# A decoder layer on one NeuronCore: reversed queries with bias tiles read from the head's own row, two accumulating transfers tied to a later split, and a sum of squares on another engine

## The chip, the cores and the metric

The kernel runs on one core of a Trainium2 chip. The metric is the device time of one execution in microseconds, the median of several runs. The core has five engines that run their own instruction streams: TensorE (PE, matmuls; PEld is its weight load), VectorE (DVE), ScalarE (ACT), GpSimd (POOL) and SyncE (SP), which only issues transfers. Transfers run on 16 DMA engines that serve several queues: q0 is fed by POOL, q1 by SP, q10 by ACT. Engines wait for each other through semaphores. On each engine the instructions are carried out in the order in which they stand.

## The reference, cut to what matters

One layer: a SwiGLU feed-forward block with a factor 0.5, a mixer (a Mamba-2 group beside differential attention with a relative position bias), cross-attention into a memory of 256 tokens, a second feed-forward block, and norms between. 512 tokens, width 1024, 8 attention heads with two queries and keys of 64 each.

```python
qb = jnp.moveaxis(q.reshape(bsz, nb, Q_BLOCK, nh, 2, dh), 1, 0)      # Q_BLOCK = 128
...
    rel = k_pos[None, :] - q_pos[:, None]
    bias = jnp.transpose(rel_bias[rel_bucket(rel)], (2, 0, 1)).astype(jnp.float32)
    logits = jnp.einsum('bqhcd,bkhcd->bhcqk', q_blk, k) * scale
    logits = jnp.where(rel[None, None, None] <= 0, logits + bias[None, :, None], -jnp.inf)
    p = jax.nn.softmax(logits, axis=-1)
    w = p[:, :, 0] - lam * p[:, :, 1]
    return jnp.einsum('bhqk,bkhe->bqhe', w.astype(v.dtype), v)
...
y = y + d_skip[:, None] * xh                                         # Mamba-2 group
y = y.reshape(bsz, seqlen, SSD_WIDTH) * jax.nn.silu(z)
yg = y.reshape(bsz, seqlen, SSD_GROUPS, SSD_WIDTH // SSD_GROUPS)
yg = yg * lax.rsqrt(jnp.mean(yg * yg, axis=-1, keepdims=True) + EPS)
...
x = x + 0.5 * swiglu(rms_norm(x, norm_ffn1_w[l]), ffn1_w_in[l], ffn1_w_out[l])
```

The bias depends on the distance between query and key alone, so a head's bias is one row of 512 values by distance.

## The kernel before

Every dense product runs as three matmuls on operands split into a high and a low part: ACT writes the high part (`wh`, L155), DVE subtracts it and writes the low part (`wl`, L156), and PE multiplies high x high, high x low and low x high. Weights come from DRAM through SP into one of six buffers `wr` (512 KB each), are split into one of three `wh` and three `wl` buffers, and are used by PE. The feed-forward products use Strassen's scheme in Winograd's form on blocks of weights (B11, B12, B21, B22) and of activations.

PE, DVE and ACT are ordered by a scheduler when the program is built; SP and POOL carry out their instructions in the order in which the program writes them down. The work is written as generators that an `Order` object advances: dense products in sequence, and chains of small steps between them. `behind(list)` makes an instruction wait for the ones in the list.

**`out_blocks`** is the second matrix of a feed-forward block, for a third of its rows. It runs seven block products: `a` with B11, `e` with the first weight sum, `b` with the second weight sum (activations S2), `a` again with B21, `b` with `sums[1]` and the activations S3, `e` with B22 and S4, and `b` with the fourth weight sum and the blocks called "22". Each has two parts (`parts`), each part one weight tile and four steps of six matmuls in all two accumulators. In the first feed-forward block the weight sums are formed on the fly. The first three share one buffer per part, `t_raw[part]`: B12 + B11 by an accumulating transfer that POOL issues (L1320), then + B22 by DVE (L1330), then + B21. In the last third (`by_dma`) that last addition is an accumulating transfer too, `t4` (L1341), issued by POOL for both parts after the S3 product has been written down. `sums[1]`, B12 + B22, is an accumulating transfer of its own per part (L1320), into a `wr` buffer for the first part and into the tile `gate` for the second. Right behind `t4` on POOL's queue stands a small power (`ncol`, L363) for the memory's norm. Meanwhile SP fetches the weights of the memory's keys (`in_wck`).

**The bias.** `prepare` forms a table `rel_d` in DRAM, 8 rows of 640 values, one row for each head: 512 by falling distance and 128 of a large constant for masked keys. A row's window that starts at 127 - p is what query p of a block of 128 needs. `expand_bias` writes a head's row 128 times into `rel_z`, in rows of 641; `ask_bias` reads it back with a step of 640, so that partition p gets the window at 127 - p. The first two heads' expansions are issued by ACT in `prepare`, behind recent splits (L640 at 323.6 and 332.6 us), the other six by SP in `queries_keys` (L640 from 348.8 to 537.6 us). The bias tile is added to the scores on DVE (L776).

**Queries and head outputs.** `queries_keys` projects a head's query, splits it from PSUM with the factor -1 (`q`, L159 on ACT and L160 on DVE), then projects and splits the key, and spawns `head`, where the queries are the stationary operand of the scores. At its end the head's output is transposed back to channels x tokens in PSUM (`pot`) and split into `ya`, which `out_attn` multiplies.

**`group`** is one of four groups of the Mamba-2 part. Its two gated tiles are squared on ACT (`ysq`, L1003), POOL adds the two squares (L1005), PE sums over channels (`pn`), and DVE and POOL form the norm's row. POOL also issues the accumulating transfers that form the second feed-forward block's weight sums in DRAM (`isum`, `wsum`, L1266); some stand behind the add on its queue.

Of the kernel before, what the change touches and what calls it, by code (L numbers as in the profile page):

```python
# [11 lines left out]
F32 = mybir.dt.float32  # L12
R32 = mybir.dt.float32r
AF = mybir.ActivationFunctionType
ALU = mybir.AluOpType
AX = mybir.AxisListType

P = 128
T = 512
# [12 lines left out]
RW = 640  # L32
# [68 lines left out]
def body(tc, a, dbg=None):  # L101
    nc = tc.nc
# [8 lines left out]
    dram = ctx.enter_context(tc.tile_pool(name="dram", bufs=1, space=bass.MemoryType.DRAM))  # L111
# [7 lines left out]
    def s2(s, dt=F32, shape=(P, T)):  # L119
        if math.prod(shape[1:]) <= T // 2:  # L120
            return sp.tile(list(shape), dt, tag="s1", name=nm(s), bufs=NHALF)
        return sp.tile(list(shape), dt, tag="s2", name=nm(s))
# [4 lines left out]
    def small(s, n, bufs=None):  # L127
        return tiny.tile([P, n], F32, tag=s, name=nm(s), bufs=bufs)

    def acc(s, shape=(P, T)):  # L130
        return acc_p.tile(list(shape), F32, tag="acc", name=nm(s))

    def aux(s, shape=(P, T)):
        return aux_p.tile(list(shape), F32, tag="aux", name=nm(s))
# [5 lines left out]
    last, start, last_sum, recent, newest, newest_mm = [], [], [], [], [], []  # L140
    V, S, G = nc.vector, nc.scalar, nc.gpsimd
    od = Order()

    def mm(out, w, x, start, stop):
        od.t += (1 if w.dtype == R32 else 4) * (x.free_size() + 8) / 2400
        newest_mm[:] = [nc.tensor.matmul(out, w, x, start=start, stop=stop).ins]  # L146
# [5 lines left out]
    def split_into(hi, lo, src, scale=None):  # L152
        if scale is None:
            return (
                S.activation(hi, src, AF.Copy),  # L155
                V.tensor_tensor(lo, src, hi.bitcast(F32), ALU.subtract),  # L156
            )
        return (
            S.activation(hi, src, AF.Copy, scale=scale),  # L159
            V.scalar_tensor_tensor(lo, src, scale, hi.bitcast(F32), ALU.mult, ALU.subtract),  # L160
        )

    def split(s, src, scale=None, half=False, n=T):
        if half:
            both = s2(s, R32, (P, 2, T // 2))
            hi, lo = both[:, 0], both[:, 1]
        else:
            hi, lo = s2(s + "h", R32, (P, n)), s2(s + "l", R32, (P, n))
        last[:] = [i.ins for i in split_into(hi, lo, src, scale)]
        return hi, lo  # L170

    def load_w(src, n=D):
        raw = wp.tile([P, n], F32, tag="wr", name=nm("wr"), bufs=6)
        nc.sync.dma_start(raw, src)
        hi = wp.tile([P, n], R32, tag="wh", name=nm("wh"))
        lo = wp.tile([P, n], R32, tag="wl", name=nm("wl"))
        with ExitStack() as after:
            for i in start:
                after.enter_context(tc.issue_after(i))
            recent[:] = [i.ins for i in split_into(hi, lo, raw)]  # L180
        return hi, lo

    @contextmanager
    def behind(ins):
        with ExitStack() as after:
            for i in ins:
                after.enter_context(tc.issue_after(i))
            yield

    H = T // 2  # L190
    S1, S2, S3, S4 = "S1", "S2", "S3", "S4"
# [129 lines left out]
    def proj(ps, w, xs, ks=None):  # L321
        n = len(xs)
        for k in ks or range(n):
            mm3(ps, w, xs[k], k == 0, k == n - 1, wc=slice(k * P, (k + 1) * P))
            yield
# [268 lines left out]
    wsub = cp.tile([P, 1], F32, name="wsub")  # L594
    dskh = cp.tile([P, 8], F32, name="dskh")
    rel_d = dram.tile([8, RW], F32, name="rel_d")
    rel_z = dram.tile([8, P, RW + 1], F32, name="rel_z")

    def lambdas():
        lamv = cp.tile([P, 4, 64], F32, name="lamv")  # L600
# [16 lines left out]
    def prepare():  # L617
        rel_far = small("rel_far", 64, bufs=1)[:8]
        V.memset(rel_far, MASKED)
        yield 9.0  # L620
        prel = aux("prel", (8, T))
        for i in range(2):
            mm(prel[:, i * H : (i + 1) * H], rel_sb, hot[i], True, True)
        for c in range(T, RW, 64):
            S.dma_start(rel_d[:, c : c + 64], rel_far)
        yield 1.5
        for i in range(2):
            S.activation(hot[i][:8], prel[:, i * H : (i + 1) * H], AF.Copy, scale=-8.0)
        yield 2.0
        for i in range(2):  # L630
            S.dma_start(rel_d[:, i * H : (i + 1) * H], hot[i][:8])
        hot.clear()
        yield 6.0
        for hd in range(2):
            with behind(list(recent)):
                expand_bias(S, hd)
            yield 4.0

    def expand_bias(queue, hd):
        queue.dma_start(rel_z[hd, :, :RW], rel_d[hd : hd + 1].to_broadcast([P, RW]))  # L640

    def bc_c(t):
        return t[:, None, :].to_broadcast([P, 4, 16])
# [73 lines left out]
    ya = [None] * 8  # L717
# [16 lines left out]
    biases = {}  # L734

    def ask_bias(hd):
        biases[hd] = s2("bias")
        S.dma_start(biases[hd], bass.AP(rel_z.tensor, rel_z.offset + hd * P * (RW + 1) + P - 1, [[RW, P], [1, T]]))

    def queries_keys(hd):  # L740
        if hd == 0:
            ask_bias(0)
        if hd < 7:
            ask_bias(hd + 1)
        if hd < 6:
            expand_bias(nc.sync, hd + 2)
        pq = acc("pq")
        yield from proj(pq, load_w(a["wq"][hd]), h)
        q = split("q", pq, -1.0)
        pk = acc("pk")  # L750
        yield from proj(pk, load_w(a["wk"][hd]), h)
        kq = split("k", pk)
        od.spawn(head(hd, q, kq, biases.pop(hd)), W["h0"])

    def head(hd, q, kq, bias):
# [77 lines left out]
        pt = aux("ptk")  # L833
# [14 lines left out]
        pt = aux("pot")  # L848
        for b in range(4):
            transpose(pt[:, b * P : (b + 1) * P], on[:, b])  # L850
        ya[hd] = split("ya", pt, wsub)
        dump(f"ya_{hd}", ya[hd][0])

    wcv = []
# [57 lines left out]
    def group(g, bt, ct, xs, zs):  # L912
# [13 lines left out]
        for c2 in range(2):  # L926
            pt = aux("pxt", (P, 2, 256))
# [37 lines left out]
        for j in range(2):  # L965
# [3 lines left out]
            for hh in range(2):  # L969
                hd = 4 * g + 2 * j + hh  # L970
# [28 lines left out]
        sq = []  # L999
        for j in range(2):  # L1000
# [1 line left out]
            q_ = s2("ysq")  # L1002
            S.activation(q_, yz[j], AF.Square)  # L1003
            sq.append(q_)
        G.tensor_tensor(sq[0], sq[0], sq[1], ALU.add)  # L1005
        yield W["gq"] + (1.2 if g == 2 else 0.0)
        pn = aux("pn", (P, 4))
        for b in range(4):
# [5 lines left out]
        for j in range(2):  # L1014
            n = 2 * g + j
# [253 lines left out]
    def out_blocks(blocks, sums, g, col4, ncol4, each=None, finale=None, clean=True, n=None, by_dma=False):  # L1269

        early = n is not None
        n = n or len(g)
# [30 lines left out]
        def product(ps, of, which, first=False, ready=None):  # L1303
            for part in parts:
                w = ready if ready and part == parts[0] else weights(of, part)
                for t in range(2):
                    yield from some(ps[t], w, which, part, t, first)
# [7 lines left out]
        t_raw = {}  # L1315
# [24 lines left out]
        def t4(part):  # L1340
            G.dma_start(t_raw[part], blocks[B21][:, part[0] * T : part[1] * T], accum_op=ALU.add)  # L1341
# [3 lines left out]
        if here:  # L1345
            sums = [t1, added(blocks[B12], blocks[B22], "gate"), t2, lambda part: t_raw[part]]
# [7 lines left out]
        b_ps = [bank[t]("ob") for t in range(2)]  # L1354
# [23 lines left out]
        later.clear()  # L1378
        for t in range(2):
            update(t, 0, a_ps[t])  # L1380
        yield from product(b_ps, sums[1], S3)
        for part in t_raw if by_dma else ():
            t4(part)
        for t in range(2):
            update(t + 2, 1, b_ps[t], -1)
        if finale is None:
# [172 lines left out]
```

## Time and profile before

| | us |
|---|---|
| runs | 1311.63, 1313.32, 1312.29; median 1312.29 |
| profiled execution | 1312.46 |
| its span, first to last instruction | 1310.7 |
| granted TensorE clock in it | 0.998 |

A row of a timeline has start and duration in us, engine, line of the kernel, operation, output and inputs by the program's names, and in brackets how long the engine was idle before and what ended it. A row of the chain of waits has start, duration and what the chain consisted of. A transfer's landing is the time from its issue to its completion.

### The profile page before, as it was taken

To read this page: it belongs to the slowest core of one execution; us is meant where nothing else is said; L and a number is where in the kernel's file an instruction comes from. 1 tells how busy PE (TensorE), PEld (TensorE's weight loads), DVE (VectorE), ACT (ScalarE), POOL (GpSimd) and SP (SyncE) were. 2 spreads that over 40 slices of the span, in tenths; PEclk is the share of its full clock that TensorE was granted. 3 is DMA by queue.
4 is the path that set the end of the run, shared out by engine and by line. 5 is a ranking of instruction groups with operands and counts; after the bars stand their busy time and mean duration, and the time that the engine had idled before them with its cause. 6 is when DMAs were issued, how large, how long until landed. Compare 5 with 4: busy or idle time off the path is not lost.

```text
span 1310.7 us, 20079 instructions
## 1 busy us (share of the span) xinstructions
PE 1287.7 (98%) x7709; PEld 1123.3 (86%) x7709; DVE 970.1 (74%) x1538; ACT 707.8 (54%) x1208; POOL 127.1 (10%) x153
## 2 busy tenths in 40 slices
PE   9999999999999999999999999999999999999997
PEld 7879998997787778777788878888889999989995
DVE  6977897797775676557867686645668878877886
ACT  7545564565754564346645465434365646555564
POOL 0001010001010011101003022020001000000000
PEclk9999999999999999999999999999999999999999
DMA  9367777776984434763466548684139876656652
GB/s 339 94 171 182 203 192 212 223 200 187 291 294 146 137 65 131 256 171 105 92 185 174 177 138 239 191 222 126 66 100 272 207 232 179 189 194 180 188 200 94
DMA packets 70415, 237.38 MB, mean 181 GB/s; under 512 B 8288, under 2 KB 9792, under 8 KB 69968
## 3 DMA queue, kind: packets, MB, share of 16 engines
q1 hardware_dynamic: 54064, 182.87, 41.1%
q0 software_dynamic: 13168, 45.67, 19.4%
q10 hardware_dynamic: 3088, 7.56, 1.6%
q8 instruction: 60, 0.98, 0.3%
q14 instruction: 35, 0.29, 0.1%
HBM read 233.92 MB, written 50.91 MB: 217 GB/s over the span
## 4 chain that ended last, share of the span: by engine, by line
PE 59%; issue 11%; DVE 3%; ACT 2%; DMA 1%; POOL 1%; POOLq 0%; ACTq 0%; DVEq 0%
PE pm L146 10%; PE qb L243 8%; PE qe L243 5%; PE qa L243 5%; PE pxbc L146 4%; PE ob L1300 4%; PE pcq L146 3%; PE pz L146 3%; PE oe L1300 2%; PE oa L1300 2%; PE pcv L146 2%; PE pq L146 2%; PE pv L146 1%; PE pk L146 1%; DMA gate<-in_f1b 1%
## 5 line engine op out<-in xcount | busy, mean ns | idle before, releaser
L155 ACT ACTIVATE wh<-wr 128x1024 fp32r<-128x1024 f32 (+1 forms) x323 | 328.4, 1020 | 355.7 <-issue 75.6
L156 DVE TENSOR_TENSOR wl<-wr,wh 128x1024 fp32r<-128x1024 f32 (+1 forms) x323 | 377.8, 1173 | 142.4 <-ACT wh L155 136.1
L777 ACT ACTIVATE ec<-ec,mn 128x512 f32<-128x512 f32 (+3 forms) x64 | 35.3, 554 | 33.7 <-DVE mn L776 33.7
L146 PE MATMUL pxbc<-hnh,wh 128*128 128x512 f32 x128 | 52.6, 411 | 0.0
L146 PE MATMUL pxbc<-hnh,wl 128*128 128x512 f32 x128 | 50.2, 393 | 0.0
L146 PE MATMUL pxbc<-hnl,wh 128*128 128x512 f32 x128 | 50.2, 392 | 0.0
L243 PE MATMUL qb<-s31h,wh 128*128 128x256 f32 x152 | 43.2, 284 | 3.2 <-ACT u L302 3.2
L243 PE MATMUL qb<-s24h,wh 128*128 128x256 f32 x152 | 43.1, 284 | 1.3 <-ACT qb L287 1.3
L243 PE MATMUL qa<-h11h,wh 128*128 128x256 f32 x152 | 43.1, 283 | 0.0
L243 PE MATMUL qa<-hmh,wh 128*128 128x256 f32 x152 | 43.0, 283 | 0.0
L243 PE MATMUL qa<-hml,wh 128*128 128x256 f32 x152 | 43.0, 283 | 0.0
L243 PE MATMUL qe<-s24h,wh 128*128 128x256 f32 x152 | 43.0, 283 | 0.0
L243 PE MATMUL qe<-s24l,wh 128*128 128x256 f32 x152 | 43.0, 283 | 0.0
L243 PE MATMUL qe<-s24h,wl 128*128 128x256 f32 x152 | 43.0, 283 | 0.0
L243 PE MATMUL qb<-hmh,wh 128*128 128x256 f32 x152 | 43.0, 283 | 0.0
L243 PE MATMUL qb<-hml,wh 128*128 128x256 f32 x152 | 43.0, 283 | 0.0
L243 PE MATMUL qb<-hmh,wl 128*128 128x256 f32 x152 | 43.0, 283 | 0.0
L243 PE MATMUL qa<-h11h,wl 128*128 128x256 f32 x152 | 43.0, 283 | 0.0
L243 PE MATMUL qb<-s24l,wh 128*128 128x256 f32 x152 | 43.0, 283 | 0.0
L243 PE MATMUL qb<-s24h,wl 128*128 128x256 f32 x152 | 43.0, 283 | 0.0
L243 PE MATMUL qa<-h11l,wh 128*128 128x256 f32 x152 | 43.0, 283 | 0.0
L243 PE MATMUL qa<-hmh,wl 128*128 128x256 f32 x152 | 43.0, 283 | 0.0
(457 smaller groups left out, 4169.9 us busy)
## 6 DMA issues: line engine op xcount, KB each, us to landing
wr<-in_f2q SPq DMA_DIRECT2D x44, 512.0 KB, 4.3
wr<-in_f1q SPq DMA_DIRECT2D x40, 512.0 KB, 4.4
wr<-in_f1b SPq DMA_DIRECT2D x25, 512.0 KB, 5.3
isum<-in_f2q SPq DMA_DIRECT2D x22, 512.0 KB, 5.2
wr<-isum SPq DMA_DIRECT2D x22, 512.0 KB, 5.1
wsum<-in_f2b SPq DMA_DIRECT2D x20, 512.0 KB, 6.2
wr<-wsum SPq DMA_DIRECT2D x20, 512.0 KB, 4.7
wr<-in_f1q POOLq DMA_DIRECT2D x16, 512.0 KB, 5.9
```

Of the source, the lines that this page charges most:

```text
L146: newest_mm[:] = [nc.tensor.matmul(out, w, x, start=start, stop=stop).ins]
L155: S.activation(hi, src, AF.Copy),
L156: V.tensor_tensor(lo, src, hi.bitcast(F32), ALU.subtract),
L243: newest_mm[:] = [nc.tensor.matmul(out, a_[:, wc], b_, start=first and f == 0 and kp == 0 and j == 0, stop=kp == n - 1 and j == 2, skip_gr ...
L777: S.activation(ec[:, :n], ec[:, :n], AF.Exp, bias=mn, scale=-1.0, accum_out=sm[c][:, i : i + 1])
L1300: newest_mm[:] = [nc.tensor.matmul(ps, a_[:, ts], b_[:, ws], start=first and k == 0 and j == 0, stop=k == n - 1 and j == 2, skip_group_che ...
```

## The change

Three edits. (1) `rel_z` and `expand_bias` go. `ask_bias` reads partition p's window from the head's row in `rel_d` at offset p, so partition p holds the bias of query 127 - p. To match, the query tile is split through `backwards`, which reads each run of 128 tokens in PSUM from its end to its start, and the head's output is split through it again, which restores the order. (2) In `out_blocks`, `t4` is written down after the first step of the S3 product's second part, and is tied to the split of that product's first part on ACT and DVE. (3) The squares of a group are added on DVE.

```diff
@@ setup @@
-    rel_z = dram.tile([8, P, RW + 1], F32, name="rel_z")
@@ prepare @@
             S.dma_start(rel_d[:, i * H : (i + 1) * H], hot[i][:8])
         hot.clear()
-        yield 6.0
-        for hd in range(2):
-            with behind(list(recent)):
-                expand_bias(S, hd)
-            yield 4.0
-
-    def expand_bias(queue, hd):
-        queue.dma_start(rel_z[hd, :, :RW], rel_d[hd : hd + 1].to_broadcast([P, RW]))
@@ ask_bias, queries_keys @@
-        S.dma_start(biases[hd], bass.AP(rel_z.tensor, rel_z.offset + hd * P * (RW + 1) + P - 1, [[RW, P], [1, T]]))
+        S.dma_start(biases[hd], bass.AP(rel_d.tensor, rel_d.offset + hd * RW, [[1, P], [1, T]]))
+
+    def backwards(t):
+        n = t.free_size()
+        return bass.AP(t.tensor, t.offset + P - 1, [list(t.ap[0]), [P, n // P], [-1, P]])
...
-        if hd < 6:
-            expand_bias(nc.sync, hd + 2)
         pq = acc("pq")
         yield from proj(pq, load_w(a["wq"][hd]), h)
-        q = split("q", pq, -1.0)
+        q = split("q", backwards(pq), -1.0)
@@ head @@
-        ya[hd] = split("ya", pt, wsub)
+        ya[hd] = split("ya", backwards(pt), wsub)
@@ group @@
-        G.tensor_tensor(sq[0], sq[0], sq[1], ALU.add)
+        V.tensor_tensor(sq[0], sq[0], sq[1], ALU.add)
@@ out_blocks @@
-        yield from product(b_ps, sums[1], S3)
-        for part in t_raw if by_dma else ():
-            t4(part)
+        for n, _ in enumerate(product(b_ps, sums[1], S3)):
+            if n == 0:
+                first_split = list(recent)
+            elif n == 4 and by_dma:
+                with behind(first_split):
+                    for part in t_raw:
+                        t4(part)
+            yield
```

Apart from the rows that the diff takes out or moves, the order on every engine stays as it was. On POOL the `t4` rows keep their place behind the gate's accumulating transfer; only what they wait for changes.

On ACT in `out_blocks` of the last third, where the S2, B21 and S3 products' weights are split (`wh`), the memory is prepared (`hm`) and new rows of x are squared (`junk`). Before:

```order
L155 ACTIVATE wh_3568<-wr_3566 128x1024
L640 DMA rel_z<-rel_d 128x640
L1373 ACTIVATE u_628_3539<-ob_3413 128x512
L155 ACTIVATE wh_3593<-wr_3590 128x1024
L1373 ACTIVATE u_629_3542<-ob_3414 128x512
L159 ACTIVATE hm_3560<-mem_542_3045,par 128x256
L159 ACTIVATE hm_3582<-mem_543_3046,par 128x256
L159 ACTIVATE hm_3606<-mem_543_3046,par 128x256
L155 ACTIVATE wh_3619<-gate_3616 128x1024
L640 DMA rel_z<-rel_d 128x640
L554 ACTIVATE junk_3612,squares_230<-x_111 128x512
```

and now:

```order
L155 ACTIVATE wh_3567<-wr_3565 128x1024
L1366 ACTIVATE u_628_3538<-ob_3412 128x512
L155 ACTIVATE wh_3591<-wr_3588 128x1024
L1366 ACTIVATE u_629_3541<-ob_3413 128x512
L159 ACTIVATE hm_3559<-mem_542_3044,par 128x256
L159 ACTIVATE hm_3580<-mem_543_3045,par 128x256
L159 ACTIVATE hm_3604<-mem_543_3045,par 128x256
L155 ACTIVATE wh_3617<-gate_3614 128x1024
L554 ACTIVATE junk_3610,squares_230<-x_111 128x512
```

The two expansions are gone; the S3 set's two splits (`wh<-wr` between the `u` rows, `wh<-gate`) stand as before, with nothing else between them.

On DVE in group 2, beside the attention output projection (`x<-x,pm`), with the gated tile (`y`), the low part of a weight split (`wl`), the memory's second copy (`hm`) and the next group's convolution (`conv`). Before:

```order
L1001 TENSOR_TENSOR y_7880<-y_7880,th_1594_7616 128x512
L156 TENSOR_TENSOR wl_8032<-wr_8029,wh_8031 128x512
L160 SCALAR_TENSOR_TENSOR hm_7891<-mem_7741,par,hm_7891 128x256
L885 SCALAR_TENSOR_TENSOR conv_7900<-pxbc_7837,par,conv_7900 128x511
L863 TENSOR_TENSOR x_121<-x_121,pm_8035 128x512
```

and now:

```order
L994 TENSOR_TENSOR y_7871<-y_7871,th_1594_7607 128x512
L156 TENSOR_TENSOR wl_8023<-wr_8020,wh_8022 128x512
L998 TENSOR_TENSOR ysq_7876<-ysq_7876,ysq_7879 128x512
L160 SCALAR_TENSOR_TENSOR hm_7882<-mem_7732,par,hm_7882 128x256
L878 SCALAR_TENSOR_TENSOR conv_7891<-pxbc_7828,par,conv_7891 128x511
L856 TENSOR_TENSOR x_121<-x_121,pm_8026 128x512
```

The add of the squares (`ysq`) stands between the split and `hm`, two rows ahead of the read of the projection's accumulator.

## The prediction

> **What bounds the kernel now.** I read the page's head and busy times first.
>
> ```profile
> span 1310.7 us, 20079 instructions
> PE 1287.7 (98%) x7709; PEld 1123.3 (86%) x7709; DVE 970.1 (74%) x1538; ACT 707.8 (54%) x1208; POOL 127.1 (10%) x153
> ```
>
> PE is busy for 98% of the span and the change removes no matmul, so work taken from DVE, ACT, POOL or a queue is worth something only where PE stands still. I went through PE's starts for pauses. Most lie where no edit reaches. Two lie beside the edits. The first is in the last third of the first feed-forward block, in `out_blocks`, where PE runs the S3 product (`ob<-s31`). PE's timeline, start and duration ahead of the name:
>
> ```profile
> 328.61 0.39 PE L1300 MATMUL oa<-wl,gh 128*128 128x512 f32 x1
> 329.04 0.50 PE L1300 MATMUL ob<-wh,s31h 128*128 128x512 f32 x1
> 329.37 0.40 PE L1300 MATMUL ob<-wh,s31l 128*128 128x512 f32 x1
> 330.30 0.50 PE L1300 MATMUL ob<-wl,s31h 128*128 128x512 f32 x1 [0.53 <-DVE wl L156]
> ...
> 332.48 0.40 PE L1300 MATMUL ob<-wl,s31h 128*128 128x512 f32 x1
> 333.70 0.50 PE L1300 MATMUL ob<-wh,s31h 128*128 128x512 f32 x1 [0.82 <-ACT wh L155]
> 334.04 0.40 PE L1300 MATMUL ob<-wh,s31l 128*128 128x512 f32 x1
> 334.96 0.50 PE L1300 MATMUL ob<-wl,s31h 128*128 128x512 f32 x1 [0.53 <-DVE wl L156]
> ```
>
> The chain of waits over the same stretch says what PE waited for:
>
> ```profile
> 319.31 13.17 DMA gate<-in_f1b
> ...
> 332.59 1.06 ACT wh L155
> ...
> 333.68 1.24 DVE wl L156
> ...
> 342.97 5.44 PE ob L1300 x24
> ```
>
> The last row gives the undisturbed pitch, 5.44/24 = 0.227 us from start to start. The four jumps above are 0.43, 0.93, 1.22 and 0.92 us, so PE loses 3.50 - 4 x 0.227 = 2.59 us: 0.91 on the first half of the set's weights (`wr`) and 1.69 on the second (`gate`). The second loss is the landing of an accumulating transfer, 332.49, plus the two halves of its split.
>
> The second pause is in the attention output projection, beside group 2's squares:
>
> ```profile
> 769.62 0.39 PE L146 MATMUL pm<-yah,wl 128*128 128x512 f32 x1
> 771.20 0.50 PE L146 MATMUL pm<-yah,wh 128*128 128x512 f32 x1 [1.19 <-DVE x L863]
> ```
>
> Here PE loses 1.58 - 0.23 = 1.35 us until DVE has emptied an accumulator. 2.59 + 1.35 = 3.94 us is all that I find within the edits' reach.
>
> **The change, part by part.** *Bias tiles.* Eight writes of an expanded row to DRAM go, two issued by ACT and six by SP, and the eight bias reads now go to the row itself. What shared the 16 DMA engines before the first landing (323 to 327.5) and then up to the second (326 to 332.5), by queue:
>
> ```profile
> q10 hardware_dynamic: 3, 0.00, 0.2%
> ...
> q0 software_dynamic: 214, 0.80, 61.5%
> q1 hardware_dynamic: 194, 0.73, 29.7%
> q10 hardware_dynamic: 144, 0.33, 12.9%
> ```
>
> q0 carries POOL's accumulating transfers, q1 SP's loads, q10 is ACT's: here the first expansion, 128 rows of 2.5 KB. It took no part in the first landing (0.2%), so I gain 0 there. In the second it held 12.9% of 6.5 us, 0.84 us of every engine, and the engines were full. Without it the gate's landing comes up to 0.84 us earlier, at 331.65; the first matmul then starts at 332.86 against 332.71 without a wait, and the whole second loss falls by that 0.84 us. Bounds: 0, if the loads of q1 take the freed time, and 0.84 by sharing alone.
>
> The other seven removals I price at nothing: the second expansion on ACT starts at 332.6, behind the gate's landing, and SP's six fall where PE waits for no weights. The new read has the old one's 128 rows of 2 KB. That they all lie in one 2.5 KB row is no new situation: the expansions read that row 128 times each. What ACT's two expansions took to land, and what the splits of the query and the key cost (count, shortest/median/longest ns, first and last start):
>
> ```profile
> DMA to landing us min/median/max: 9.1/9.2/9.3
> L159 ACT ACTIVATE qh<-pq x8: 575/582/594, 381.9 to 620.2; 128x512 fp32r<-128x512 f32 x8
> L160 DVE SCALAR_TENSOR_TENSOR ql<-pq,qh x8: 680/683/689, 383.2 to 622.3; 128x512 fp32r<-128x512 f32 x8
> L155 ACT ACTIVATE kh<-pk x8: 577/580/588, 387.9 to 627.1; 128x512 fp32r<-128x512 f32 x8
> ```
>
> A bias tile is asked for one head before its use, so even a landing after the expansions' 9.3 us is covered. Sixteen splits (query and head output, 8 heads) now read PSUM backwards in runs of 128, on ACT and on DVE; no row has such a step. The same count of elements at the same price is the near bound; the far one is twice: 0.58 us more on ACT and 0.68 on DVE for a query tile. The key projection covers it: the key split starts 387.9 - 381.9 = 6.0 us after the query's, and the scores need both. I take 0. The Trainium skill's Vector Engine (DVE) Microarchitecture Reference, section 5.1, counts the streaming of an operand with a negative step among what was not measured; no run here shows it yet.
>
> *Running sums' transfers.* The two accumulating transfers of L1341 keep their place on POOL's queue but gain a wait for the S3 set's first split on ACT and DVE. Before, they were issued at 319.9 and 321.8 and landed 16.4 and 19.9 us later:
>
> ```profile
> L1341 POOL DMA_DIRECT2D wr<-in_f1b x2: 863/1040/1218, 319.9 to 321.8; - x2
> ...
> DMA to landing us min/median/max: 16.4/18.2/19.9
> ```
>
> That is 336.3 and 341.7, behind the `wr` and the gate that went out ahead of them at 318.1 and 319.3 and took 9.7 and 13.2:
>
> ```profile
> L1320 POOL DMA_DIRECT2D wr<-in_f1b x1: 863/863/863, 318.1 to 318.1; - x1
> ...
> DMA to landing us min/median/max: 9.7/11.4/13.2
> L1320 POOL DMA_DIRECT2D gate<-in_f1b x1: 866/866/866, 192.8 to 192.8; - x1
> ...
> DMA to landing us min/median/max: 5.7/6.7/7.7
> ```
>
> (The last two lines are the same place in the second third, where no L1341 follows: there the gate landed 7.7 us after its issue, here 13.2.) Four landings in order of issue, 327.8, 332.5, 336.3, 341.7, look like one line in which the later transfers wait rather than share. Then taking them out of the line helps the gate by 0; if they did share, by up to what is left of the two losses, 2.59 - 0.84 = 1.75 us. I take 0, from the order of landings; the second third speaks for more, but no expansion ran beside it either.
>
> The price is a later landing. The new release and who else stands in POOL's line:
>
> ```profile
> 329.02 1.23 DVE L156 TENSOR_TENSOR wl<-wr,wh 128x1024 fp32r<-128x1024 f32 x1 [3.48 <-PE oa L1300]
> 322.35 2.15 POOL L363 TENSOR_TENSOR ncol<-nv,mhalf 128x2 f32<-128x2 f32 x1
> 336.62 0.16 DVE L368 CAST ch<-ncol 128x2 fp32r<-128x2 f32 x1
> ```
>
> The split ends at 330.25, so the transfers go out at about 330.3 and 331.2. The memory's `ncol` behind them then ends near 332.2 + 2.15 = 334.4; DVE asks for it at 336.62, 2.2 us later, so it stays covered. The sums are due when the "22" product starts (342.97); its second half starts 12 x 0.227 later, at 345.69. With the 1.29 us gained below, 344.40. From a landing to the end of DVE's split are 334.96 - 332.49 = 2.47 us, and DVE's part is asked for by the third matmul, 0.45 later: the second sum has to land by 342.4. The bytes to move are the same less the two expansions, so I expect 340 to 342, as before: 0. The bad end: 13.2 us from issue, the gate's under load, is 344.4, a loss of 2.0 us.
>
> *Squares.* Four adds move from POOL to DVE. At group 2, POOL's row first:
>
> ```profile
> 768.32 1.29 POOL L1005 TENSOR_TENSOR ysq<-ysq,ysq 128x512 f32<-128x512 f32 x1 [44.80 <-ACT ysq L1003]
> 764.11 0.48 DVE L160 SCALAR_TENSOR_TENSOR hm<-mem,par,hm 128x256 fp32r<-128x256 f32 x1
> 764.50 0.55 DVE L993 TENSOR_TENSOR y<-y,e 128x384 f32<-128x384 f32 x1
> ...
> 767.75 0.69 DVE L156 TENSOR_TENSOR wl<-wr,wh 128x512 fp32r<-128x512 f32 x1 [1.96 <-ACT wh L155]
> 768.67 1.23 DVE L160 SCALAR_TENSOR_TENSOR hm<-mem,par,hm 128x256 fp32r<-128x256 f32 x1 [0.23 <-ACT hm L159]
> 769.82 0.73 DVE L885 SCALAR_TENSOR_TENSOR conv<-pxbc,par,conv 128x511 f32<-128x511 f32 x1
> 770.48 0.67 DVE L863 TENSOR_TENSOR x<-x,pm 128x512 f32<-128x512 f32 x1
> ```
>
> While POOL adds, DVE's `hm` takes 1.23 us, not 0.48. With the add on DVE, right behind `wl`: add at 768.35 (0.69 by the equal-sized `wl`, next start 0.6 on), `hm` at 768.95 (next start 0.4 on, as at 764.11 before its successor), `conv` at 769.35, the emptying at 770.03 instead of 770.48. PE gains 0.45 us; the bounds are a loss of 0.6, if `hm`'s length had another cause, and the whole 1.35. At the other groups DVE stands idle for over a microsecond soon after and PE waits for nothing: 0. POOL's sum transfers behind the adds go out earlier, where nobody waits.
>
> Sum: 0.84 + 0 + 0.45 = 1.29 us. The profiled execution took 1312.46 us, 1.8 of it outside the span, 0.17 above the median of 1312.29; 1312.29 - 1.29 = **1311.0 us**.
>
> **Rivals.** (A) *The gate lands much earlier*, since what went out behind it did share, or since ACT's writes held its completion. For it: 7.7 us against 13.2, and the expansion issued at 323.6 lands 9.1 us later at 332.7, with the gate. Against it: the landings in line. Then nearly all of 2.59 goes, with 0.45: 1312.29 - 3.04 = 1309.3. The Trainium skill's DMA: Bandwidth & Descriptors, section Queues, rings and completion order, has a completion write land only after every earlier write of that engine, over all its queues, which would tie the gate to the expansion in this way; the trace agrees in the times but cannot tell it from sharing.
> (B) *The sums land late*, the wait in place of the one removed: at 344.4 as worked out, +2.0: 1313.0, slower. It decides once the second sum lands after 343.7, 1.29 us past due. For it: transfers that POOL issues among SP's loads took 9.7 and 13.2 us.
> (C) *Only the squares count*: q1 takes the freed time, and nothing else moves: 1312.29 - 0.45 = 1311.8.
> (D) *Backward reads are slow* by a factor n, not by two at most. Against it: nothing but the lack of a row. A query's two splits then take (n - 1) x (0.58 + 0.68) us more, and from 6.0 us on, at n = 5.8, they hold the scores; at n = 8 that is 8.8 - 6.0 = 2.8 us a head, 22 us for eight: 1333, slower.
>
> **How the numbers follow.** Forecast 0.47, A 0.27, C 0.11, B 0.11, D 0.04. What a measurement can tell from no change is about 0.2%, 2.6 us: below 1309.7 faster, above 1314.9 slower. A lies mostly below (0.24), the forecast's tail adds 0.04: faster 0.28. Slower: D 0.04, B's tail and what I have not thought of 0.04. Same 0.64. The range runs from just past A, 1308.8, to just past B, 1313.2; the forecast's own is 1310.2 to 1311.9.
>
> **What would show it.** In the profile after: no ACT queue traffic between 323 and 333; the gate's landing near 331.7 and PE's second S3 pause near 0.85 us, the first near 0.9 as before; L1341 issued near 330.3, landing at 340 to 342 and no pause in the "22" product; `hm` beside group 2's add at 0.48 and PE's pause there near 0.9; `qh` and `yah` as long as before. Wrong: the gate at 330 or sooner (A), a pause in "22" or at the memory's `ch` (B), reversed splits over 1.2 us (D).

## The result, and the profile after

| | before | after |
|---|---|---|
| median of the runs on one chip, us | 1313.04 (21 runs, 1311.27 to 1314.07) | 1310.9 (21 runs, 1309.76 to 1312.98) |
| ratio | | 0.9986, 95% interval 0.998 to 0.9992 |
| profiled execution, us | 1312.46 | 1310.42 |
| its span, us | 1310.7 | 1308.6 |
| granted TensorE clock | 0.998 | 0.997 |

The change makes the kernel faster by 0.14%, between 0.08 and 0.2%: 1.8 us by the ratio, with bounds of 1.1 and 2.6, and 2.1 us between the two medians. The page of the profile after, head and busy times:

```profile
span 1308.6 us, 20067 instructions
PE 1287.1 (98%) x7709; PEld 1123.3 (86%) x7709; DVE 971.6 (74%) x1542; ACT 707.9 (54%) x1208; POOL 121.4 (9%) x149
```

DVE has four instructions more and POOL four fewer, the moved adds; PE's work is the same. So the time came from PE's pauses. First the last third's S3 product, PE's timeline after:

```profile
328.10 0.39 PE L1293 MATMUL oa<-wl,gh 128*128 128x512 f32 x1
328.33 0.40 PE L1293 MATMUL ob<-wh,s31h 128*128 128x512 f32 x1
328.57 0.40 PE L1293 MATMUL ob<-wh,s31l 128*128 128x512 f32 x1
329.48 0.50 PE L1293 MATMUL ob<-wl,s31h 128*128 128x512 f32 x1 [0.52 <-DVE wl L156]
...
331.66 0.39 PE L1293 MATMUL ob<-wl,s31h 128*128 128x512 f32 x1
332.08 0.50 PE L1293 MATMUL ob<-wh,s31h 128*128 128x512 f32 x1
332.42 0.39 PE L1293 MATMUL ob<-wh,s31l 128*128 128x512 f32 x1
333.34 0.50 PE L1293 MATMUL ob<-wl,s31h 128*128 128x512 f32 x1 [0.53 <-DVE wl L156]
```

Less the pitch of 0.227 us, the four jumps are 0.00, 0.69, 0.20 and 0.69: 1.6 us against 2.59 before. The large one, PE waiting for the high part of the `gate` weights, fell from 0.99 to 0.20. The gate's transfer and who used the DMA engines from 326 to 332.5 us, after:

```profile
gate<-in_f1b POOLq DMA_DIRECT2D x1, 512.0 KB, 12.0
```

```profile
q0 software_dynamic: 246, 0.90, 69.1%
q1 hardware_dynamic: 239, 0.91, 37.1%
```

ACT's queue (q10) is gone from this stretch, where it held 12.9%, and both others hold more than before (61.5 and 29.7%). The gate landed 12.0 us after its issue instead of 13.2.

POOL's timeline over the same stretch shows the step that went another way than foreseen:

```profile
318.84 0.86 POOL L1313 DMA_DIRECT2D gate<-in_f1b  x1 [0.35 <-ACT hm L159]
319.38 1.22 POOL L1334 DMA_DIRECT2D wr<-in_f1b  x1
321.31 0.87 POOL L1334 DMA_DIRECT2D wr<-in_f1b  x1 [0.71 <-ACT wh L155]
```

The running sums' transfers, which should have waited for the S3 set's first split until 330, went out at 319.38 and 321.31, right behind the gate's as before.

DVE's timeline beside group 2's squares, after:

```profile
766.12 0.69 DVE L156 TENSOR_TENSOR wl<-wr,wh 128x512 fp32r<-128x512 f32 x1 [1.95 <-ACT wh L155]
766.73 0.68 DVE L998 TENSOR_TENSOR ysq<-ysq,ysq 128x512 f32<-128x512 f32 x1
767.33 0.48 DVE L160 SCALAR_TENSOR_TENSOR hm<-mem,par,hm 128x256 fp32r<-128x256 f32 x1
767.73 0.74 DVE L878 SCALAR_TENSOR_TENSOR conv<-pxbc,par,conv 128x511 f32<-128x511 f32 x1
768.43 0.69 DVE L856 TENSOR_TENSOR x<-x,pm 128x512 f32<-128x512 f32 x1
```

and PE beside it:

```profile
768.00 0.39 PE L146 MATMUL pm<-yah,wl 128*128 128x512 f32 x1
769.17 0.50 PE L146 MATMUL pm<-yah,wh 128*128 128x512 f32 x1 [0.78 <-DVE x L856]
```

From `wl` to the emptying of the accumulator (`x<-x,pm`) DVE now takes 768.43 - 766.12 = 2.31 us, before 770.48 - 767.75 = 2.73. PE's pause is 1.17 - 0.23 = 0.94 us instead of 1.35.

Last the reversed splits, after (shortest/median/longest ns):

```profile
L159 ACT ACTIVATE qh<-pq x8: 576/582/592, 380.3 to 618.6; 128x512 fp32r<-128x512 f32 x8
L160 DVE SCALAR_TENSOR_TENSOR ql<-pq,qh x8: 681/684/690, 381.6 to 620.7; 128x512 fp32r<-128x512 f32 x8
L159 ACT ACTIVATE yah<-pot,wsub x8: 671/678/690, 428.5 to 661.7; 128x512 fp32r<-128x512 f32 x8
L160 DVE SCALAR_TENSOR_TENSOR yal<-pot,wsub,yah x8: 744/748/752, 429.2 to 662.4; 128x512 fp32r<-128x512 f32 x8
```

The query's medians are 582 and 684 ns against 582 and 683 before, and the head output's before were:

```profile
L159 ACT ACTIVATE yah<-pot,wsub x8: 669/677/690, 430.1 to 663.3; 128x512 fp32r<-128x512 f32 x8
L160 DVE SCALAR_TENSOR_TENSOR yal<-pot,wsub,yah x8: 744/748/751, 430.8 to 664.0; 128x512 fp32r<-128x512 f32 x8
```

Reading these PSUM runs of 128 from end to start costs nothing here, on either engine.

The spans differ by 2.1 us. The S3 product's pauses give 1.0 of it (1.1 with the starts just behind them, which also stand further apart than the pitch), group 2 gives 0.41. Another 0.7 is a pause at 88 us, in the first third, ahead of everything that the change touches:

```profile
88.34 0.39 PE L1300 MATMUL ob<-wh,s31l 128*128 128x512 f32 x1
90.06 0.50 PE L1300 MATMUL ob<-wl,s31h 128*128 128x512 f32 x1 [1.34 <-DVE wl L156]
```

is the profile before, with 1.72 us between the starts; in the profile after these are 1.06 us apart. Over the eleven profiles of the table below that jump less the pitch lies between 0 and 1.50 us, with the same instructions in the same order up to it, so this part of the difference between the two spans is scatter and not the change's.

### The profile page after: what moved, and what is told of

Its sections match the earlier page's. It is cut to its first block, busy times and chain, and to the rows that moved or that the text cites. A ratio compares the mean times of both kernels' runs of the same rounds, so it can differ in the third digit from the quotient of the medians.

```text
span 1308.6 us, 20067 instructions
## 1 busy us (share of the span) xinstructions
PE 1287.1 (98%) x7709; PEld 1123.3 (86%) x7709; DVE 971.6 (74%) x1542; ACT 707.9 (54%) x1208; POOL 121.4 (9%) x149
## 4 chain that ended last, share of the span: by engine, by line
PE 58%; issue 13%; DVE 2%; ACT 2%; POOL 1%; POOLq 0%; ACTq 0%; DVEq 0%
PE pm L146 10%; PE qb L243 8%; PE qe L243 5%; PE qa L243 5%; PE pxbc L146 4%; PE pcq L146 3%; PE ob L1293 3%; PE pz L146 3%; PE oa L1293 3%; PE oe L1293 2%; PE pcv L146 2%; PE pq L146 2%; PE pv L146 1%; PE pk L146 1%; PE pcs L146 1%
## 5 line engine op out<-in xcount | busy, mean ns | idle before, releaser
L243 PE MATMUL qb<-s31h,wl 128*128 128x256 f32 x152 | 43.0, 283 | 0.0
```

Source lines behind the costliest of these rows:

```text
L243: newest_mm[:] = [nc.tensor.matmul(out, a_[:, wc], b_, start=first and f == 0 and kp == 0 and j == 0, stop=kp == n - 1 and j == 2, skip_gr ...
```

## The experiments

The kernels' times lie within 2.5 us of each other and single runs of one kernel scatter by as much and more, so the theories were told apart by the profile: the gate's landing and PE's pauses. Here are the eleven profiles in which the S3 product stands at its old place, side by side ("pauses" is the sum of the same four jumps, each less the pitch and taken from the trace's nanoseconds; "group 2" is the jump beside the squares):

| kernel | ACT's queue beside the gate | gate, issue to landing | S3 pauses | group 2 |
|---|---|---|---|---|
| before | 2 expansions | 13.17 | 2.59 | 1.35 |
| the tie alone | 2 expansions | 12.68 | 2.12 | 1.35 |
| squares alone | 2 expansions | 13.17 | 2.46 | 0.94 |
| expansions put back | 2 expansions | 13.03 | 2.58 | 0.94 |
| row read to SBUF | reads of 1 KB rows | 12.92 | 2.31 | 0.94 |
| row written to DRAM | copies of 1 KB rows | 12.52 | 2.05 | 0.94 |
| after | nothing | 12.02 | 1.59 | 0.94 |
| bias tiles alone | nothing | 11.74 | 1.41 | 1.35 |
| a real wait | nothing | 12.12 | 1.56 | 0.94 |
| no add | nothing | 11.63 | 1.30 | 0.94 |
| early reads | a late read, 2.0% | 11.97 | 1.49 | 0.94 |

Each row is one profile. Of the four jumps, the one in which PE waits for the high part of the `gate` weights parts the kernels best: 0.89 to 1.00 us with ACT's two expansions, 0.48 and 0.53 with the 1 KB rows, 0.18 to 0.21 with nothing or the late read.

**Bias tiles alone.** The kernel before with edit (1) and nothing else (the first hunk's removals, `ask_bias`, `backwards`).

```diff
-    rel_z = dram.tile([8, P, RW + 1], F32, name="rel_z")
...
-        S.dma_start(biases[hd], bass.AP(rel_z.tensor, rel_z.offset + hd * P * (RW + 1) + P - 1, [[RW, P], [1, T]]))
+        S.dma_start(biases[hd], bass.AP(rel_d.tensor, rel_d.offset + hd * RW, [[1, P], [1, T]]))
...
-        q = split("q", pq, -1.0)
+        q = split("q", backwards(pq), -1.0)
```

> The kernel before with the bias edit alone (head's own row, reversed queries and outputs). Theory (the pause ahead of and inside the S3 product shrinks because ACT's first expansion no longer shares the DMA engines): PE's loss on S3 falls from 2.59 us to 1.2 to 1.7, gate's accumulating transfer lands 12.0 us after its issue (13.2 before), group 2's pause stays at 1.35 us, time 1.0 to 1.5 us under before, ratio 0.9989 to 0.9992. Rival (the tie of the running sums' transfers has a part in it): PE's loss on S3 stays at 2.2 or more, time within 0.5 us of before.

1311.5 us, ratio 0.9996 (0.9988 to 1.0005), where the theory had 0.9989 to 0.9992. The gate landed after 11.74 us and the pauses fell to 1.41, as the theory had it; group 2 stayed at 1.35. The time alone tells it neither from nothing nor from the expected gain.

**The tie alone.** The kernel before with edit (2).

```diff
-        yield from product(b_ps, sums[1], S3)
-        for part in t_raw if by_dma else ():
-            t4(part)
+        for n, _ in enumerate(product(b_ps, sums[1], S3)):
+            if n == 0:
+                first_split = list(recent)
+            elif n == 4 and by_dma:
+                with behind(first_split):
+                    for part in t_raw:
+                        t4(part)
+            yield
```

> The kernel before with the running sums' transfers written down later and tied to the S3 set's first split, nothing else. Theory (the tie makes POOL wait for nothing): the two transfers still go out near 319.9 and 321.8 us, ahead of the split near 328, PE's loss on S3 stays at 2.3 to 2.9 us, ratio 0.9996 to 1.0004. Rival (the tie helps the gate's landing): loss on S3 under 1.9 us, at least 0.7 us faster.

1312.28 us, ratio 0.9999, 0.9991 to 1.0008. POOL's timeline:

```profile
319.17 0.87 POOL L1320 DMA_DIRECT2D gate<-in_f1b  x1 [0.36 <-ACT hm L159]
319.70 1.22 POOL L1341 DMA_DIRECT2D wr<-in_f1b  x1
321.70 0.87 POOL L1341 DMA_DIRECT2D wr<-in_f1b  x1 [0.78 <-ACT wh L155]
```

The tie is no wait here either. (The list does name the S3 set's first split: the real wait below takes its tile at the same place of the program, and that wait holds until 329.8 us.) The pauses of 2.12 us lie a little under those of the other kernels with expansions and above the 1.9 from which the rival counted; as the two transfers went out when they always did, the edit gives no reason for a gain, and I count the 0.4 as scatter.

**Squares alone.** The kernel before with edit (3).

```diff
-        G.tensor_tensor(sq[0], sq[0], sq[1], ALU.add)
+        V.tensor_tensor(sq[0], sq[0], sq[1], ALU.add)
```

> The kernel before with the squares added on VectorE, nothing else. Theory: the hm beside group 2's add takes 0.48 us instead of 1.23, PE's pause there falls from 1.35 to 0.9 us, the S3 loss stays at 2.3 to 2.9, time 0.4 us under before, ratio 0.9995 to 0.9999. Rival (the add on VectorE costs more than the port's conflict): the pause grows by up to 0.6 us.

1312.12 us, ratio 1.0, 0.9991 to 1.0009. Group 2's pause is 0.94 as in the changed kernel, with `hm` at 0.48 us, and the S3 product's pauses stay at 2.46. In the profiles the two gains are separate. The run times alone don't show it: the three edits have ratios of 0.9996, 0.9999 and 1.0 one by one, each known to about 0.0009, and 0.9986 together. That the gain is made of these two parts rests on the pauses.

**S4 ahead of S3.** A try at a better kernel: the changed kernel, in the first block with the S4 product, whose weights come by a plain load, ahead of S3, whose weights are late.

```diff
...
+            ahead = {part: sums[1](part) for part in parts}
+            for part in t_raw if by_dma else ():
+                t4(part)
+            yield from product(e_ps, b22, S4)
...
+            yield from product(b_ps, ahead.get, S3)
...
```

> The changed kernel with the S4 product run ahead of the S3 product in the first feed-forward block, transfers issued in the same order as before. Theory (PE's losses on S3 are lateness of accumulating transfers alone, and plain fetches for S4 are there in time): no pause inside S3 or S4 in the last third and near 88 us; the second running sum lands near 339.5 us and is due near 340.2, so the last product waits at most 0.5 us; against before 1.6 us of the change + 1.4 + 0.8 = 3.8 us, ratio 0.9967 to 0.9977. Rival (the wait moves to the last product or to S4's splits): as much pause there as S3 loses now, ratio 0.9983 to 0.9989.

1312.82 us, ratio 1.0006, 0.9996 to 1.0016: no gain, though all pauses of the S3 product are gone. PE's timeline shows where they went:

```profile
340.44 0.39 PE L1293 MATMUL ob<-wl,s31h 128*128 128x512 f32 x1
340.67 0.38 PE L150 MATMUL pxf<-ident,x 128*128 128x128 f32 x2
342.50 0.47 PE L1293 MATMUL ob<-wh,gh 128*128 128x512 f32 x1 [1.45 <-DVE x L1304]
```

S3 and "22" both accumulate in `ob`, and with S4 no longer between them nothing covers the emptying of `ob`. DVE's timeline:

```profile
340.46 1.23 DVE L156 TENSOR_TENSOR wl<-wr,wh 128x1024 fp32r<-128x1024 f32 x1 [2.55 <-ACT wh L155]
341.61 1.40 DVE L1304 SCALAR_TENSOR_TENSOR x<-ob,ncol,x 128x512 f32<-128x512 f32 x2
```

The wait moved to the last product (and waits of 0.5 and 0.7 us came up in the same block's earlier thirds), as the rival had it, though PE waits for its accumulator and not for its weights. The late weights have a share in it all the same: DVE starts to empty `ob` at 341.61, 0.8 us after S3's last matmul ends, because it first splits the second half of the last product's weights, which had landed at 339.3. How much each is worth was not tried. The ratio is above what either theory had.

**A real wait.** The changed kernel with a copy on POOL of one column of the S3 set's first low part ahead of the running sums' transfers.

```diff
+            newest_w[:] = [hi, lo]
...
-                first_split = list(recent)
+                first_split = list(newest_w)
...
-                with behind(first_split):
-                    for part in t_raw:
-                        t4(part)
+                G.tensor_copy(small("tie", 1), first_split[1][:, 0:1].bitcast(F32))
+                for part in t_raw:
+                    t4(part)
```

> The changed kernel, with the wait made real: ahead of the running sums' two accumulating transfers POOL copies one column of the S3 set's first low part (128x1, never read again), which it can do only once DVE has written it (about 329.5 to 330.2 us). In the changed kernel and with the tie alone the transfers went out at 319.4 to 319.7, before that split. All theories: they now go out at 330 to 331.5. Theory (POOL's transfers are served in line, later ones cost the earlier nothing): the set's first and second landing stay at 9.0 to 9.8 and 11.6 to 12.6 us after issue, the S3 pauses at 1.2 to 1.7 us, the second sum lands by 342.5 and the last product pauses by under 0.5 us; ratio to the kernel before 0.9985 to 0.9995. Rival A (they share the engines with the gate): gate in under 11 us, S3 pauses under 0.8 us. Rival B (the sums land late under the other loads): the second sum lands after 343.5 and the last product pauses by 0.8 to 3 us; ratio 0.9995 to 1.002.

1311.66 us, ratio 0.9992, 0.9983 to 1.0001. POOL's timeline and the landings of the two transfers:

```profile
319.10 0.86 POOL L1316 DMA_DIRECT2D gate<-in_f1b  x1 [0.35 <-ACT hm L159]
329.83 0.19 POOL L1381 COPY tie<-wl 128x1 f32<-128x1 f32 x1 [9.87 <-DVE wl L156]
330.32 1.76 POOL L1337 DMA_DIRECT2D wr<-in_f1b  x2 [0.30 <-ACT hm L159]
```

```profile
L1337 POOL DMA_DIRECT2D wr<-in_f1b x2: 866/1038/1210, 330.3 to 330.9; - x2
...
DMA to landing us min/median/max: 8.7/9.7/10.7
```

Now they wait. With 1 MB less behind it for 11 us, the gate landed after 12.12 us, as in the changed kernel (12.02), and the pauses are 1.56 against 1.59: what stands behind the gate on POOL's queue takes nothing from it. Nor did SP's loads take up time that had come free, which would have hidden a gain: from 326 to 329 us, while the gate was under way, POOL's queue moved 0.38 MB and SP's 0.45 MB with the real wait, 0.40 and 0.44 MB in the changed kernel. The second sum landed at 330.87 + 10.7 = 341.6, 2.0 us later than in the changed kernel (321.31 + 18.2), and the last product did not pause; 0.3 us of PE's idle time appeared in the transposes behind it, behind DVE's updates. The theory held, rivals A and B fell, and the wait that the diff speaks of gains nothing even when it is one.

**The expansions put back.** The changed kernel with ACT's two expansions at their old places, into a table that nothing reads.

```diff
+    rel_z = dram.tile([8, P, RW + 1], F32, name="rel_z")
...
+        yield 6.0
+        for hd in range(2):
+            with behind(list(recent)):
+                S.dma_start(rel_z[hd, :, :RW], rel_d[hd : hd + 1].to_broadcast([P, RW]))
+            yield 4.0
```

> The changed kernel with ACT's two expansions put back where they stood (each 128 rows of 2.5 KB from DRAM to DRAM), into a table that nothing reads. Theory (they take time of the engines that carry the gate): the gate lands 12.6 to 13.3 us after its issue instead of 12.0, the S3 pauses are 2.1 to 2.7 us instead of 1.6; ratio to the kernel before 0.999 to 1.0003. Rival (the gain came from the reads or the other six writes): gate under 12.2 us, S3 pauses under 1.7 us.

1312.2 us, ratio 0.9999, 0.9989 to 1.0008. The gate's transfer and ACT's share from 326 to 332.5 us:

```profile
gate<-in_f1b POOLq DMA_DIRECT2D x1, 512.0 KB, 13.0
```

```profile
q10 hardware_dynamic: 139, 0.33, 12.9%
```

13.03 us and pauses of 2.58: the whole loss is back, with the reads of the bias still straight from the row and the six writes of SP still gone. The S3 product's gain is that of these two transfers. The second goes out at 332.8, behind the gate's landing at 332.7, so it is the first that counts.

**Early reads.** Meant to tell sharing from a completion that stands behind writes to DRAM: reads of the bias tiles by ACT in place of the expansions.

```diff
+        yield 6.0
+        for hd in range(2):
+            with behind(list(recent)):
+                ask_bias(hd)
+            yield 4.0
...
-        if hd == 0:
-            ask_bias(0)
-        if hd < 7:
+        if 0 < hd < 7:
             ask_bias(hd + 1)
```

> The changed kernel, in which ACT issues the first two heads' bias reads (128 rows of 2 KB, DRAM to SBUF) where the kernel before issued its two expansions (128 rows of 2.5 KB, DRAM to DRAM). Nearly the same bytes come in, and no write to DRAM is left. Theory of sharing (bytes on the engines delay the gate): the gate lands 12.4 to 13.1 us after its issue, the S3 pauses are 2.0 to 2.6 us. Rival (it was the writes to DRAM, behind which the gate's completion stood): gate 11.7 to 12.2 us, S3 pauses 1.2 to 1.7 us as in the changed kernel.

1310.78 us, ratio 0.999, 0.9981 to 0.9999. The gate landed after 11.97 us, which is what the rival had, but the run doesn't count for it: ACT's timeline shows the read 4.5 us later than the expansion's 323.6, behind the first split.

```profile
327.90 1.06 ACT L155 ACTIVATE wh<-wr 128x1024 fp32r<-128x1024 f32 x1 [4.23 <-DMA wr<-in_f1b]
328.06 0.35 ACTq L734 DMA_DIRECT2D bias<-rel_d  x1
```

ACT's share from 326 to 332.5 us:

```profile
q10 hardware_dynamic: 25, 0.05, 2.0%
```

What was to stand beside the gate was hardly there.

**The row to SBUF, and the same to DRAM.** Two kernels that differ in the destination alone: 512 values of the row, 128 times, as two transfers of 1 KB rows at each of the expansions' places. (`held` are the two tiles `hot`, made 128 rows high for it in both kernels.)

```diff
...
+                for i in range(2):
+                    S.dma_start(held[i], rel_d[hd : hd + 1, i * H : (i + 1) * H].to_broadcast([P, H]))
...
```

> The changed kernel in which ACT, at the places of its two former expansions, reads 512 values of the head's row 128 times into SBUF, into two tiles that nothing reads again, as two transfers of 128 rows of 1 KB. The early reads' run told nothing, since its read went out at 328.1 us instead of 323.6. The reads into the tiles here are written down right behind the same split as the expansions. Theory of sharing (time of the engines): the gate lands 12.6 to 13.2 us after its issue and the S3 set loses 2.5 to 3.1 us, as with the expansions (before 13.17 and 3.10, with the expansions put back 13.03 and 3.09). Rival (the completion stands behind writes to DRAM): 11.6 to 12.1 us and 1.6 to 2.0 us, as in the changed kernel (12.02 and 1.98).

and for the second

```diff
-                    S.dma_start(held[i], rel_d[hd : hd + 1, i * H : (i + 1) * H].to_broadcast([P, H]))
+                    S.dma_start(rel_z[hd, :, i * H : (i + 1) * H], rel_d[hd : hd + 1, i * H : (i + 1) * H].to_broadcast([P, H]))
```

> The run before with the same transfers (128 rows of 1 KB, two at a place, the same source, issue and order) written to DRAM, into a table that nothing reads, instead of to SBUF. Sharing: the gate 12.6 to 13.2 us after its issue, within 0.3 us of the run that writes to SBUF, and the S3 set loses 2.5 to 3.1 us. Rival (writes to DRAM hold the completion): 12.6 to 13.2 us here too, but 0.7 us or more above the run that writes to SBUF.

1312.92 us, ratio 1.0005 (0.9995 to 1.0014), and 1311.51 us, ratio 0.9994 (0.9985 to 1.0004). Into SBUF, the gate and ACT's share from 326 to 332.5 us:

```profile
gate<-in_f1b POOLq DMA_DIRECT2D x1, 512.0 KB, 12.9
```

```profile
q10 hardware_dynamic: 218, 0.21, 9.4%
```

and into DRAM:

```profile
gate<-in_f1b POOLq DMA_DIRECT2D x1, 512.0 KB, 12.5
```

```profile
q10 hardware_dynamic: 212, 0.20, 9.0%
```

From the start ahead of the set to the set's last, less the pitch, the S3 set lost 2.80 and 2.54 us, where the theory had 2.5 to 3.1. Both delay the gate, by 1.0 and 0.6 us over the mean of 11.9 of the five kernels without such traffic, and the one with no write to DRAM at least as much. That the landing stood behind writes to DRAM is out. Time on the engines, 9.4 and 9.0% of 6.5 us, makes 0.6 us in both, all of the second delay but not all of the first. The first transfer went out some 2 us earlier here than the expansion (321.9), so the sizes are not to be compared to a tenth of a us. The second gate's 12.52 lies 0.1 under the theory's range, and the two runs differ by 0.4 us, 0.1 more than the theory allowed. That is of the size of the scatter (11.63 to 12.12 without such traffic), and it goes against the rival.

Run times part in the same way, though not cleanly: ratios of 0.9986 to 0.9996 in the five kernels with nothing or only the late read on ACT's queue, 0.9994 to 1.0005 in the five with traffic there.

**No add.** The changed kernel without the add; the norm leaves out the second tile's squares.

```diff
-        V.tensor_tensor(sq[0], sq[0], sq[1], ALU.add)
```

> The changed kernel without the add of the two tiles' squares in the four groups: the norm leaves out the second tile. Prices the add on DVE apart from the port. Theory (of the 0.94 us that PE still pauses at group 2, the add is the next part on DVE's path): the pause falls by 0.45 to 0.65 us, to 0.3 to 0.5, and the memory's copy stays at 0.48 us. Rival (DVE waits there for ACT's copy and the add is free): the pause stays above 0.8 us. Ratio to the kernel before 0.9982 to 0.999.

1310.9 us, ratio 0.9991, 0.9982 to 1.0. The pause stayed at 0.94 us: the theory fell and the rival held. DVE's timeline:

```profile
765.96 0.69 DVE L156 TENSOR_TENSOR wl<-wr,wh 128x512 fp32r<-128x512 f32 x1 [1.95 <-ACT wh L155]
766.88 0.49 DVE L160 SCALAR_TENSOR_TENSOR hm<-mem,par,hm 128x256 fp32r<-128x256 f32 x1 [0.23 <-ACT hm L159]
767.55 0.75 DVE L878 SCALAR_TENSOR_TENSOR conv<-pxbc,par,conv 128x511 f32<-128x511 f32 x1 [0.18 <-ACT conv L875]
768.26 0.69 DVE L856 TENSOR_TENSOR x<-x,pm 128x512 f32<-128x512 f32 x1
```

Without the add DVE stands idle for 0.23 us until ACT has written `hm` and for 0.18 until ACT has written `conv`, and empties the accumulator 2.30 us after `wl`, as with the add (2.31). The add fills time in which DVE waited for ACT, so it costs nothing at this place. What the edit brought is `hm` at 0.48 us instead of 1.23.

## Why the prediction was right, and where a step was not

The predicted 1311.0 us lies 0.1 from the measured median, and a distance that small is luck: the kernel before measured 1313.04 in the same runs and not the 1312.29 that I started from, so the change brought 2.1 us by the medians (1.8 by the ratio, 1.1 to 2.6), and I had predicted 1.29. A start that was 0.75 us too low and a gain that was 0.85 too small cancel. The pauses of the profiles give 1.4; what the rest of the 2.1 is, no run shows.

- *The first expansion beside the gate, 0.84 us.* Right in place and nearly in size: the loss on the second half, which the term prices, fell from 1.69 to 0.89, by 0.80. The expansions put back brought that loss back. (The gate landed at 330.9 and not near 331.65, 0.5 us of it because it went out earlier, at 318.84.) All four pauses together fell by 1.0 between the two profiles, and by 0.97 between the means of the four kernels with ACT's expansions (2.44) and the four with nothing on ACT's queue (1.47). The difference lies in the first half, where I had written "I gain 0 there": its two jumps were 0.90 before and 0.69 after, but between 0.54 and 0.90 with expansions and between 0.41 and 0.69 without, so a few tenths may belong to the change. The mechanism is shown in part. ACT's traffic delays the gate, wherever it is written to; but the gate came 1.15 us sooner after its issue (1.1 between the means), more than the 0.84 that I gave as the bound "by sharing alone". What makes up the rest stays open.
- *Seven further transfers and the new reads at nothing.* Nothing shows against it: with only ACT's two back, gate and pauses were those of before. The second of these two was not tried apart.
- *The reversed reads at 0.* Right, to 1 ns in 582 and 684. Rival D falls, and with it the doubled price that I kept as the far bound. The Trainium skill's Vector Engine (DVE) Microarchitecture Reference, section 5.1, counts how the engine streams an operand with a negative step among what was not measured; here it ran as fast as forward, 684 against 683 ns.
- *"They keep their place but gain a wait; the transfers go out at about 330.3 and 331.2."* This step failed. They went out at 319.38 and 321.31 and landed at 334.6 and 339.5. In the text ahead of the prediction I had written that `behind` makes an instruction wait for those in its list; for an instruction on POOL with a list on ACT and DVE it made none, in the changed kernel and with the tie alone (319.70 and 321.70). The sum was not hurt, since I had priced the wait at 0 from the order of landings, and the run in which the wait is real confirms that price: gate unchanged, second sum at 341.6 where I expected 340 to 342. Rival B's 344.4, from the gate's 13.2 us under load, was 2.5 us too late: issued at 330 the transfers took 8.7 and 10.7 us.
- *The squares at 0.45.* 0.41 measured, in the changed kernel and alone, and with the chain on DVE as laid out (emptying 2.28 us behind `wl` by the prediction, 2.31 measured). The bound of a loss, "if `hm`'s length had another cause", is out: the same instruction took 1.23 us beside POOL's add and 0.47 to 0.49 in the nine profiles without it. The Trainium skill's SBUF — State Buffer, section Who interferes with whom, calls the pair of ports that DVE and GpSimd share an exclusive lock; 1.23 against 0.48 us, with the end 0.3 us behind the end of POOL's add, agrees with it.
- *Rivals A and C.* A needed the gate at 330 or sooner and nearly no pauses; the gate landed at 330.9 and 1.6 us of pauses stayed, 1.4 of them PE waiting for DVE's half of the two splits. C is out by the expansions put back.

The Trainium skill's DMA: Bandwidth & Descriptors, section Queues, rings and completion order, has each DMA engine take turns between the queues that have work for it. The runs agree: traffic of ACT's queue delayed POOL's transfer by 0.6 to 1.3 us, while what POOL itself issued behind it delayed it by nothing (12.12 us without, 12.02 with). The same section of the Trainium skill has a completion land only behind every earlier write of its engine, over all its queues; no run here could exclude that, since reads into SBUF end in writes too. The engine time of ACT's traffic, 0.6 to 0.84 us, falls short of most of the delays, so whether sharing is all of it stays open.

## What to carry to other kernels

Look at what shares the DMA engines with the transfer whose landing the tensor engine waits for: a small transfer on another queue, of 0.6 to 0.84 us of engine time, delayed it here by 0.6 to 1.3 us, while later transfers on its own queue could be left where they were. Before pricing a wait that a source line seems to add, see in the built program or in the trace whether the instruction has it: here a list of instructions on ACT and DVE held nothing on POOL. And price an instruction added to an engine by its idle time at that place: an add of 0.68 us cost nothing where the engine otherwise stood idle for 0.41 us (2.31 us from `wl` to the emptying with it, 2.30 without), and the gain came from its neighbour, which was 0.75 us shorter once POOL no longer added beside it.

## What had not been expected of the hardware

- The landing followed the issue only in part for transfers in this loaded line: the running sums' transfers, issued 11 and 9.6 us later, landed 4.4 and 2.0 us later (339.0 and 341.6 against 334.6 and 339.5).
- Code that the change doesn't touch scatters between single profiles by as much as the change is worth: the jump at 88 us took between 0 and 1.50 us over its pitch, for the same instructions in the same order. Ahead of it an accumulating transfer of POOL (`wr`, issued at 77 to 78 us) landed after 7.0 us in the profile without the jump and after 9.3 in the one with the longest.
- A swap that takes all 1.6 us of pauses out of one product can gain nothing: 1.45 us came back one product later, where an accumulator that had been emptied under cover no longer was.
